# One core, two layers of mixers and feed-forward: the last mixers in two streams before retention, the second output projection in block pairs, operand sums on POOL, another pool order

## The chip, the cores and the metric

The kernel runs on one core of a Trainium2 chip. The metric is device time in microseconds, the median of several runs. One execution of the program is also profiled; its trace gives every instruction's start and duration. TensorE is called PE, VectorE DVE, ScalarE ACT, GpSimd POOL and SyncE SP. SP issues most of the transfers; the code of the other engines sees them through semaphores.

## The reference

Two layers over 1024 tokens of width 1024. A layer is four token mixers side by side, an output projection, and a gated feed-forward with a causal convolution over three tokens:

```python
h = rms_norm(x, g_pre_mix)
p = h @ w_in
a_pool, r_q, r_k, r_v, r_g, s_u, s_v, d_qkv, d_z, d_b, d_a = jnp.split(p, IN_SPLITS, axis=-1)
y_a = pool_mixer(a_pool, pool_w, pool_scale)
y_b = retention_mixer(r_q, r_k, r_v, r_g, cos, sin)
y_c = spatial_gating_mixer(s_u, s_v, sgu_ln_g, sgu_ln_b, sgu_ws, sgu_bs)
y_d = deltanet_mixer(d_qkv, d_z, d_b, d_a, dn_conv_w, dn_a_log, dn_dt_bias, dn_norm_g)
y = jnp.concatenate([y_a, y_b, y_c, y_d], axis=-1)
x = x + rms_norm(y @ w_out, g_post_mix)
h = rms_norm(x, g_pre_ffn)
x = x + rms_norm(conv_ffn(h, ffn_w_up, ffn_conv_w, ffn_conv_b, ffn_w_down), g_post_ffn)
```

Retention multiplies queries and keys (turned by rope) within chunks of 128 tokens and carries a state from chunk to chunk. The delta-net solves a unit lower triangular system of 64 tokens for each chunk and head, and carries a state through the chunks. Both are short dependent chains of small products; the projections, up and down are large products.

## The kernel before

All is in float32. A large product is made of three products of rounded parts: an operand is split into hi (a cast, on ACT) and lo (the difference, on DVE), and hi x hi, hi x lo and lo x hi are added in PSUM. A weight tile of 512 KB is loaded into one of two raw buffers and split by `unit` (L187 to L202). `a_unit` multiplies it with the transposed rows of 512 tokens in 24 matmuls (L210 to L212); `b_units` uses two such weight tiles for four blocks of 128 tokens (L231 to L233).

The tokens are taken in two halves of 512. The order of all instructions on each engine is fixed beforehand by the framework's scheduler, which simulates the program; `high_priority` shifts what it wraps towards an earlier place in that order. An engine then takes its instructions one by one: one that waits holds all behind it on this engine, and SP's transfers the same.

The part of the program that matters here begins with the last mixers, those of layer 1 and the second half of the tokens.

- `win` runs the projections and mixers in the order of the letters in ORD: among others u (the projections of retention's q, k, v), n (retention's gate), r (retention) and b (the delta-net's end).
- `retention` turns q and k by rope (DVE L630 and L634, POOL L633), then runs four blocks with the state `ret`. With FAST for the first mixers of the program (layer 0, first half) it runs two blocks by turns.
- `dn_back` inverts the triangular 32 x 32 parts: 31 steps on DVE, each a product and a sum (L831, L833), a transfer to memory and back (SP L835 to L866), then for each of four blocks a solve (L874 to L912) and a scan (L936 to L961). Without FAST solve and scan of a block come one after another; with FAST `turns` lets generators run by turns: two solves together, then scans 0 and 1 beside solves 2 and 3, then scans 2 and 3.
- `plain_up` makes up tiles f = 0 to 7 of layer 1 for the first half of the tokens: five before the output projection and three behind it. Its rows are transposed and split by `to_hT` (L365 to L369).
- `out` projects the mixers' output by `wO`, and `norms` adds the residual, norms again and stores the result to `hnD`.
- `build` loads rows from `hnD`, makes the seven transposed operands A11, A12, A22, S1, S2, S3, Q4 of a product scheme with seven instead of eight block products; one call takes one half of the tokens. `up_f` then makes an up tile with seven products, for one half (256 columns) or both. f = 0 to 7 are made for the second half alone, since `plain_up` made the first. Up tiles go to memory in `gD`.
- `down_full` loads them again (`graw`), splits them, loads the down weights (raw, `in_wD`), and adds up all in `acc`; `end_block` norms a block, adds x (`xb`, issued by POOL at L1207) and stores it.

`phase` opens the tile pools of a part of the program; a pool of a later phase that lies where an earlier one lay waits for that one's tiles. So the order of the pools sets which old tile a new one waits for.

Of the kernel before, what the change touches and what calls it, by code (L numbers as in the profile page):

```python
# [9 lines left out]
F32 = mybir.dt.float32  # L10
# [4 lines left out]
ALU = mybir.AluOpType  # L15
# [18 lines left out]
ORD0 = "unszrpqgfb"  # L34
ORD = "zspgqunrb"
HP0 = {"r": 500, "b": 300}
HP1 = {}
# [79 lines left out]
class Net:  # L117
# [30 lines left out]
    def down_phase(self):  # L148
        self.phase(("pw", 6), ("pg", 6), ("pa", 8), ("pr", 2), ("py", 2))

# [70 lines left out]

    def b_units(self, aps, hT, width, n):
        us = [self.unit(ap, 4 * width) for ap in aps]
        for b in range(NB):
            ps = self.ps()
            for k in range(len(hT)):
                hi, lo = us[k // 4]
                s = slice((k % 4) * width, (k % 4 + 1) * width)
                tb = slice(b * P, b * P + P)
                h0, h1 = hT[k][0][:, tb], hT[k][1][:, tb]  # L230
                self.nc.tensor.matmul(ps[:, :width], h0, hi[:, s], start=k == 0, stop=False)  # L231
                self.nc.tensor.matmul(ps[:, :width], h0, lo[:, s], start=False, stop=False)  # L232
                self.nc.tensor.matmul(ps[:, :width], h1, hi[:, s], start=False, stop=k == len(hT) - 1)  # L233
            yield b, ps
# [72 lines left out]

    def norms(self, raw, hn, gpost, gpre, src, dst, keep=None):
        nc = self.nc
        for b in range(NB):  # L310
            xb = self.py.tile([P, D], F32, tag="xb", name="xb")
# [106 lines left out]
    def win(self, l, h, hT, pre=None):  # L418
# [105 lines left out]
        def do_ret():  # L524
            self.retention(l, h, R["rqk"], R["rv"], R["rg"], FAST and (l, h) == (0, 0))

        def do_back():
            self.dn_back(l, qf, R["zf"], sc, dn, FAST and (l, h) == (0, 0))

# [3 lines left out]
        steps = dict(n=do_rg, f=do_first, z=do_z, s=do_su, p=do_pool, g=do_sgu, q=do_pmix, u=do_runits, r=do_ret, b=do_back)  # L533
        for k in (ORD0 if (l, h) == (0, 0) else ORD):
            off = dict(HP0 if (l, h) == (0, 0) else HP1).get(k)
            if off:
                with self.tc.high_priority(offset=off):
                    steps[k]()
            else:
                steps[k]()  # L540
# [424 lines left out]
    def out(self, l, h, y, mid=False, halves=False):  # L965
# [18 lines left out]
        gpost = self.bcast(t["gB"][4 * l + 1], "zf" if mid else "gpost", pool=alt if mid else None)  # L984
        gpre = self.bcast(t["gB"][4 * l + 2], "ap" if mid else "gpre", pool=alt if mid else None)
        for kh in range(2 if halves else 1):
            for q in range(4):
# [4 lines left out]
                for b, ps in self.b_units(aps, yT[4 * kh:4 * kh + 4 * len(aps)], 256, 4):  # L992
                    with self.tc.high_priority(offset=HPE):
                        if kh == 0:
                            nc.scalar.copy(raw[b][:, s], ps[:, :256])
                        else:
                            nc.vector.tensor_tensor(raw[b][:, s], raw[b][:, s], ps[:, :256], ALU.add)
        hn = raw if mid else self.acc_tiles()
        self.norms(raw, hn, gpost, gpre, src, dst, self.hnD[l][h * HALF:h * HALF + HALF] if l in FULL else None)
        return hn  # L1000
# [28 lines left out]
    def cbuf(self, name):  # L1029
        return self.pu.tile([P, 1028], F32, tag="c", name=name, bufs=4)  # L1030

# [11 lines left out]
    def build(self, l, h):  # L1043
        nc = self.nc
        V, A = nc.vector, self.A
        for i in range(2):
            cs = slice(h * 256 + i * P, h * 256 + i * P + P)
            xs = []
            for e in range(2):
# [3 lines left out]
                xs.append(x)  # L1053
            ps = []
            for e in range(2):
                for kk in range(2):
                    p = self.ps() if kk == 0 else self.pq()
                    for k in range(4):
                        c = (kk * 4 + k) * P
                        nc.tensor.transpose(p[:, k * P:k * P + P], xs[e][:, c:c + P], self.ident)  # L1060
                    ps.append(p)
            p00, p01, p10, p11 = ps
            v4 = lambda a: a.rearrange("p (k t) -> p k t", k=4)

            def put(n, src):
                hi, lo = self.A[n]
                nc.scalar.copy(hi[:, :, cs], v4(src))
                V.tensor_tensor(lo[:, :, cs], v4(src), hi[:, :, cs].bitcast(F32), ALU.subtract)

            a21, s1, s3, s2, q4 = (self.pbuf(n) for n in ("a21", "s1", "s3", "s2", "q4"))  # L1070
            put("A11", p00)
            nc.scalar.copy(a21, p10)
            V.tensor_tensor(s1, a21, p11, ALU.subtract)
            put("S1", s1)
            V.tensor_tensor(s2, s1, p00, ALU.subtract)
            put("S2", s2)
            put("A12", p01)
            V.tensor_tensor(s3, p00, a21, ALU.subtract)
            put("S3", s3)
            V.tensor_tensor(q4, s2, p01, ALU.add)  # L1080
            put("Q4", q4)
            put("A22", p11)

# [118 lines left out]
    def end_block(self, l, b, acc, gpost):  # L1202
        nc = self.nc
        V = nc.vector
        rows = slice(b * P, b * P + P)
        xb = self.py.tile([P, D], F32, tag="xb", name="xb")
        nc.gpsimd.dma_start(xb, self.xs[2 * l][rows])  # L1207
# [92 lines left out]
    def run(self):  # L1300
# [23 lines left out]
        self.build(l, 1)  # L1324
        for f in range(NHALF):
            if f == 1:
                self.build(l, 0)
            self.up_f(l, f, (1,))
        for f in range(NHALF, NF):
            self.up_f(l, f, (0, 1))  # L1330
        self.down_phase()
# [78 lines left out]
```

## Time and profile before

| | us |
|---|---|
| median of 3 runs | 2571.22 (2569.04 to 2571.54) |
| the profiled execution | 2572.25 |
| its span | 2570.5 |
| PE busy | 2444.2 (95%) |
| DVE busy | 1771.3 (69%) |
| ACT busy | 963.6 (37%) |
| POOL busy | 242.7 (9%) |

The span is the time from the first to the last record of the profiled execution. Busy times are sums over the whole span. Times in a timeline are from the span's start: start, duration, engine, line and operation, written and read tiles, and in brackets the idle time before it and what ended it. In groups the two numbers behind the bar are the sum in us and the mean of one in ns.

### The profile page before, as it was taken

The page shows a single profiled execution, that of the slowest core. Times are in us where ns is not written, and L with a number is a line of the kernel's source. Part 1 is how long each engine was busy: PE and PEld are TensorE (multiplying, and loading weights), DVE is VectorE, ACT ScalarE, POOL GpSimd, SP SyncE. Part 2 cuts the span into 40 slices and gives each one's busy share as a digit, 9 for nine tenths or more (in the row PEclk, how much of TensorE's full clock was granted, in tenths as well). Part 3 has the DMA queues.
Part 4 walks back from the last instruction along what each step waited for, and adds up shares of the span by engine and source line. Part 5 has one row for each costly group of instructions (what it writes and reads, how often), then busy time and mean ns, then how long its engine had stood idle before and what let it go on. Part 6 is the DMA issues. An engine that isn't in the chain of part 4 may idle for free. (4 is left out here: it accounts for less than half of the span.)

```text
span 2570.5 us, 36403 instructions
## 1 busy us (share of the span) xinstructions
PE 2444.2 (95%) x14068; PEld 2041.1 (79%) x14068; DVE 1771.3 (69%) x3665; ACT 963.6 (37%) x1505; POOL 242.7 (9%) x343
## 2 busy tenths in 40 slices
PE   8989998999999999999999999896968999989997
PEld 7978987877788978787788897785858888868886
DVE  7895799665655888855655687963388866653537
ACT  6343443423323462433333355231245534433212
POOL 2321112000000014000000001300000000000002
PEclk9999999999999999999999999995899999999999
DMA  5233442322233542322223453230253322233313
GB/s 181 77 90 101 140 143 79 96 72 86 87 91 128 167 148 78 89 75 83 74 91 99 148 189 132 77 104 22 66 201 115 107 86 79 82 108 106 131 66 115
DMA packets 97329, 270.34 MB, mean 105 GB/s; under 512 B 30130, under 2 KB 30450, under 8 KB 96644
## 3 DMA queue, kind: packets, MB, share of 16 engines
q1 hardware_dynamic: 93380, 255.36, 30.5%
q0 software_dynamic: 3776, 12.65, 1.6%
q8 instruction: 111, 1.82, 0.3%
q14 instruction: 62, 0.51, 0.1%
HBM read 230.19 MB, written 37.78 MB: 104 GB/s over the span
## 5 line engine op out<-in xcount | busy, mean ns | idle before, releaser
L200 ACT CAST whi<-raw 128x1024 fp32r<-128x1024 f32 (+1 forms) x290 | 302.3, 1049 | 669.8 <-PE psg L211 193.1
L211 PE MATMUL psg<-hT,whi 128*128 128x512 f32 x1280 | 509.1, 398 | 1.3 <-DVE hT L369 1.3
L210 PE MATMUL psg<-hT,whi 128*128 128x512 f32 x1280 | 508.9, 398 | 0.5 <-DVE hT L369 0.3
L212 PE MATMUL psg<-hT,wlo 128*128 128x512 f32 x1280 | 508.9, 399 | 0.0
L201 DVE TENSOR_TENSOR wlo<-raw,whi 128x1024 fp32r<-128x1024 f32 (+1 forms) x267 | 329.6, 1240 | 180.1 <-ACT whi L200 175.3
L211 PEld LDWEIGHTS psg<-hT,whi 128*128 128x128 f32 x1280 | 241.7, 189 | 57.1 <-DVE hT L369 1.9
L212 PEld LDWEIGHTS psg<-hT,wlo 128*128 128x128 f32 x1280 | 241.8, 189 | 55.8 <-issue 0.2
L210 PEld LDWEIGHTS psg<-hT,whi 128*128 128x128 f32 x1280 | 241.6, 189 | 54.8 <-ACT hT L368 0.6
L1247 DVE TENSOR_TENSOR acc<-acc,psg 128x512 f32<-128x512 f32 x160 | 109.1, 686 | 74.6 <-PE psg L1242 74.0
L232 PE MATMUL psg<-wlo,hT 128*128 128x256 f32 (+1 forms) x512 | 148.5, 291 | 5.9 <-DVE wlo L201 5.9
L231 PE MATMUL psg<-whi,hT 128*128 128x256 f32 (+1 forms) x512 | 145.8, 288 | 3.1 <-DVE rqk L510 3.0
L231 PE MATMUL psg<-whi,y 128*128 128x256 f32 x512 | 144.6, 288 | 4.1 <-ACT y L205 2.2
L233 PE MATMUL psg<-whi,hT 128*128 128x256 f32 (+1 forms) x512 | 148.0, 290 | 0.0
L232 PE MATMUL psg<-wlo,y 128*128 128x256 f32 x512 | 144.8, 285 | 0.0
L1106 ACT CAST w<-wraw 128x512 fp32r<-128x512 f32 x154 | 92.2, 619 | 138.3 <-PE psg L1092 57.7
L233 PE MATMUL psg<-whi,y 128*128 128x256 f32 x512 | 143.7, 285 | 0.0
L1240 PE MATMUL psg<-whi,g 128*128 128x512 f32 x352 | 141.5, 404 | 0.0
L1241 PE MATMUL psg<-wlo,g 128*128 128x512 f32 x352 | 138.8, 394 | 0.0
L1242 PE MATMUL psg<-whi,g 128*128 128x512 f32 x352 | 138.6, 394 | 0.0
L1107 DVE TENSOR_TENSOR w<-wraw,w 128x512 fp32r<-128x512 f32 x154 | 103.6, 688 | 46.5 <-ACT w L1106 45.3
L831 DVE SCALAR_TENSOR_TENSOR pr<-A 64x1 f32<-64x1 f32 (+30 forms) x124 | 115.2, 929 | 5.6 <-POOL A L827 3.6
L232 PEld LDWEIGHTS psg<-wlo,hT 128*128 128x128 f32 x512 | 98.1, 192 | 9.7 <-DVE wlo L201 6.9
(464 smaller groups left out, 5095.3 us busy)
## 6 DMA issues: line engine op xcount, KB each, us to landing
raw<-in_wU SPq DMA_DIRECT2D x104, 512.0 KB, 3.5
raw<-in_wD SPq DMA_DIRECT2D x66, 512.0 KB, 3.7
raw<-in_wA SPq DMA_DIRECT2D x56, 512.0 KB, 3.7
wraw<-in_wU SPq DMA_DIRECT2D x22, 1024.0 KB, 4.9
raw<-in_wO SPq DMA_DIRECT2D x32, 512.0 KB, 3.7
raw<-in_wB SPq DMA_DIRECT2D x24, 512.0 KB, 3.6
xs<-xb SPq DMA_DIRECT2D x24, 512.0 KB, 3.4
graw<-gD SPq DMA_DIRECT2D x22, 512.0 KB, 4.8
```

The costliest lines, as they stand in the source:

```text
L200: nc.scalar.copy(hi[:, :n], raw[:, :n])
L201: eng.tensor_tensor(lo[:, :n], raw[:, :n], hi[:, :n].bitcast(F32), ALU.subtract)
L210: nc.tensor.matmul(ps, a[0], b[0], start=first, stop=False)
L211: nc.tensor.matmul(ps, a[0], b[1], start=False, stop=False)
L212: nc.tensor.matmul(ps, a[1], b[0], start=False, stop=last)
L231: self.nc.tensor.matmul(ps[:, :width], h0, hi[:, s], start=k == 0, stop=False)
L232: self.nc.tensor.matmul(ps[:, :width], h0, lo[:, s], start=False, stop=False)
L233: self.nc.tensor.matmul(ps[:, :width], h1, hi[:, s], start=False, stop=k == len(hT) - 1)
L831: V.scalar_tensor_tensor(pr[:, 0:i, 0:i], A[:, 0:i, 0:i], -1.0, A[:, 0:i, i].unsqueeze(1).to_broadcast([64, i, i]), ALU.mult, ALU.mult)
L1240: nc.tensor.matmul(ps, hi[:, tb], us[i][0][:, s], start=i == 0, stop=False)
L1241: nc.tensor.matmul(ps, hi[:, tb], us[i][1][:, s], start=False, stop=False)
L1242: nc.tensor.matmul(ps, lo[:, tb], us[i][0][:, s], start=False, stop=i == len(g0) - 1)
```

## The change

- The mixers of layer 1, second half, run in the order ORD1, with b (the delta-net's end) ahead of r (retention), and both take the FAST path (two streams), as the first mixers do. In this path the scans use another PSUM pool and keep their small matrices in row buffers.
- The `out` call that stands between the plain up tiles (`mid`) runs in two passes over block pairs: blocks 0 and 1 through all weights, their norms, then blocks 2 and 3 through all weights again, and their norms. The weights are loaded and split once for each pass.
- `build` computes the four sums on POOL from the loaded rows (128 x 512 each, in buffers of its own), transposes all seven operands on PE instead of four quarters, and splits each from PSUM. The row buffers `c` are six, not four.
- f = 0 and f = 1 are made for the second half, then the other half is built, and f = 2 to 7 for the second half come between the whole tiles from f = 8 on.
- The pools of the down phase are opened in another order, `xb` of the end has six buffers, and the scratch memory for POOL's transfers is 8192.

Line numbers behind the changed lines move by a few: the delta-net's L874, L936 and L960 are L876, L938 and L962 now, the sums on POOL are L1068 to L1071, the split in `build` is L1080, and L1222 of `end_block` is L1220.

```diff
+ORD1 = "zspgqunbr"
+QUICK = ((0, 0), (1, 1))
...
     def down_phase(self):
-        self.phase(("pw", 6), ("pg", 6), ("pa", 8), ("pr", 2), ("py", 2))
+        self.phase(("pa", 8), ("pr", 2), ("py", 2), ("pw", 6), ("pg", 6))
...
-    def b_units(self, aps, hT, width, n):
+    def b_units(self, aps, hT, width, n, blocks=range(NB)):
         us = [self.unit(ap, 4 * width) for ap in aps]
-        for b in range(NB):
+        for b in blocks:
...
-            self.retention(l, h, R["rqk"], R["rv"], R["rg"], FAST and (l, h) == (0, 0))
+            self.retention(l, h, R["rqk"], R["rv"], R["rg"], FAST and (l, h) in QUICK)
...
-            self.dn_back(l, qf, R["zf"], sc, dn, FAST and (l, h) == (0, 0))
+            self.dn_back(l, qf, R["zf"], sc, dn, FAST and (l, h) in QUICK)
...
-        for k in (ORD0 if (l, h) == (0, 0) else ORD):
+        for k in (ORD0 if (l, h) == (0, 0) else ORD1 if (l, h) in QUICK else ORD):
...
+        if mid:
+            for blocks in ((0, 1), (2, 3)):
+                for q in range(4):
+                    for b, ps in self.b_units([t["wO"][l, 2 * q], t["wO"][l, 2 * q + 1]], yT, 256, 4, blocks):
+                        with self.tc.high_priority(offset=HPE):
+                            nc.scalar.copy(raw[b][:, q * 256:q * 256 + 256], ps[:, :256])
+                self.norms(raw, hn, gpost, gpre, src, dst, keep, blocks)
+            return hn
...
     def cbuf(self, name):
-        return self.pu.tile([P, 1028], F32, tag="c", name=name, bufs=4)
+        return self.pu.tile([P, 1028], F32, tag="c", name=name, bufs=6)
...
+            L, R = slice(0, 512), slice(512, 1024)
+            sa, sb = self.cbuf("sa"), self.cbuf("sb")
+            G = nc.gpsimd
+            G.tensor_tensor(sa[:, L], xs[1][:, L], xs[1][:, R], ALU.subtract)
+            G.tensor_tensor(sa[:, R], sa[:, L], xs[0][:, L], ALU.subtract)
+            G.tensor_tensor(sb[:, R], sa[:, R], xs[0][:, R], ALU.add)
+            G.tensor_tensor(sb[:, L], xs[0][:, L], xs[1][:, L], ALU.subtract)
+            for i_, (n, x, s) in enumerate((("A11", xs[0], L), ("A12", xs[0], R), ("A22", xs[1], R), ("S1", sa, L),
+                                            ("S2", sa, R), ("S3", sb, L), ("Q4", sb, R))):
+                p = (self.ps, self.pq)[i_ % 2]()
+                for k in range(4):
+                    nc.tensor.transpose(p[:, k * P:k * P + P], x[:, s][:, k * P:k * P + P], self.ident)
+                p4 = p.rearrange("p (k t) -> p k t", k=4)
                 hi, lo = self.A[n]
-                nc.scalar.copy(hi[:, :, cs], v4(src))
-                V.tensor_tensor(lo[:, :, cs], v4(src), hi[:, :, cs].bitcast(F32), ALU.subtract)
-            a21, s1, s3, s2, q4 = (self.pbuf(n) for n in ("a21", "s1", "s3", "s2", "q4"))
-            put("A11", p00)
-            nc.scalar.copy(a21, p10)
-            V.tensor_tensor(s1, a21, p11, ALU.subtract)
-            put("S1", s1)
...
+                nc.scalar.copy(hi[:, :, cs], p4)
+                V.tensor_tensor(lo[:, :, cs], p4, hi[:, :, cs].bitcast(F32), ALU.subtract)
...
-        xb = self.py.tile([P, D], F32, tag="xb", name="xb")
+        xb = self.py.tile([P, D], F32, tag="xb", name="xb", bufs=6)
...
-        for f in range(NHALF):
-            if f == 1:
-                self.build(l, 0)
+        for f in range(2):
             self.up_f(l, f, (1,))
+        self.build(l, 0)
+        half = list(range(2, NHALF))
         for f in range(NHALF, NF):
+            if half:
+                self.up_f(l, half.pop(0), (1,))
             self.up_f(l, f, (0, 1))
...
-    nc = bacc.Bacc("TRN2", target_bir_lowering=False, num_devices=1)
+    nc = bacc.Bacc("TRN2", target_bir_lowering=False, num_devices=1,
+                   dynamic_dma_scratch_size=8192)
```

PE at the delta-net, before: the last matmul of the first block's solve (L908), its scan, and the next block's solve. Ahead of these rows stand retention and five plain up tiles.

```order
L908 MATMUL psm<-R_14590,kt 64x64
L936 MATMUL psm<-S,tmp 64x64 x8
L951 MATMUL psm<-Sb,qf 64x128 x2
L954 MATMUL psm<-R_14590,AT 128x64 x2
L951 MATMUL psm<-Sb,qf 64x128 x2
L954 MATMUL psm<-R_14590,AT 128x64 x2
L960 MATMUL psm<-ident,tmp 128x128 x2
L874 MATMUL psm<-x_100,LT 32x32 x8
L882 MATMUL psm<-XT,x_100 32x32 x8
```

PE at the same place now: behind the last projection (L213, L214) and a few transposes of the rows for the plain up tiles, the first two solves begin together.

```order
L213 MATMUL psg<-hT_13390,whi 128x512
L214 MATMUL psg<-hT_13388,wlo 128x512
L367 MATMUL psg<-ident,acc_13475 128x128
L367 MATMUL psg<-ident,acc_13476 128x128 x4
L367 MATMUL psg<-ident,acc_13477 128x128 x4
L876 MATMUL psm<-x_99,LT 32x32 x8
L876 MATMUL psm<-x_100,LT 32x32 x8
L884 MATMUL psm<-XT,x_99 32x32 x8
L884 MATMUL psm<-XT,x_100 32x32 x8
L893 MATMUL psm<-R_14590,XT 128x128 x8
```

And where it ends: the last scan, the other transposes, retention's first transposes and scores (L645, L653), then the first plain up matmuls (L212).

```order
L938 MATMUL psh<-S,mc_15467 64x64 x8
L953 MATMUL psh<-Sb,qf 64x128 x2
L956 MATMUL psh<-R_14590,AT 128x64 x2
L953 MATMUL psh<-Sb,qf 64x128 x2
L956 MATMUL psh<-R_14590,AT 128x64 x2
L962 MATMUL psh<-ident,tmp 128x128 x2
L367 MATMUL psh<-ident,acc_13475 128x128 x4
L367 MATMUL psh<-ident,acc_13476 128x128 x4
L645 MATMUL psm<-ident,rqk_14975 128x128 x4
L367 MATMUL psh<-ident,acc_13477 128x128 x4
L645 MATMUL psm<-ident,rqk_14975 128x128 x4
L367 MATMUL psg<-ident,acc_13478 128x128 x4
```

The whole delta-net has moved ahead of retention and of all plain up tiles, and between its solves and scans no matmul of a plain up tile is left.

SP at the first builds, before: the last rows' store (L322), the first build's four loads, two weight loads, the second build's four.

```order
L1101 DMA wraw<-in_wU 128x2x1024
L1026 DMA gD_109<-c 128x512
L1101 DMA wraw<-in_wU 128x2x1024
L322 DMA hnD_107<-osu 128x1024
L1052 DMA hn<-hnD_107 128x1024 x4
L1101 DMA wraw<-in_wU 128x2x1024 x2
L1052 DMA hn<-hnD_107 128x1024 x4
L1164 DMA gD_109<-c 128x512
```

Now:

```order
L324 DMA hnD_107<-osu 128x1024
L1099 DMA wraw<-in_wU 128x2x1024 x2
L1037 DMA gD_109<-c 128x512
L1063 DMA hn<-hnD_107 128x1024 x2
L1099 DMA wraw<-in_wU 128x2x1024
L1063 DMA hn<-hnD_107 128x1024 x2
L1099 DMA wraw<-in_wU 128x2x1024
L1162 DMA gD_109<-c 128x512
L1063 DMA hn<-hnD_107 128x1024 x2
L1099 DMA wraw<-in_wU 128x2x1024
L1162 DMA gD_109<-c 128x512
```

The rows' stores stand before the last plain up tile's store; the loads come in pairs, with a weight load between them, and the second build's behind the first split tiles' stores.

SP from up to down, before:

```order
L1177 DMA graw<-gD_109 128x1024 x2
L1164 DMA gD_109<-c 128x1024
L198 DMA raw<-in_wD 128x1024 x2
L1177 DMA graw<-gD_109 128x1024 x2
```

The first down weights have moved behind two more loads of `graw`:

```order
L1175 DMA graw<-gD_109 128x1024 x2
L1162 DMA gD_109<-c 128x1024
L1175 DMA graw<-gD_109 128x1024 x2
L200 DMA raw<-in_wD 128x1024 x2
L1175 DMA graw<-gD_109 128x1024 x2
```

More of the change, by code (lines that the diff above doesn't have):

```diff
@@ L306, in sumsq, with norms @@
         return self.rstd(ss, 1, 1.0 / D)
-    def norms(self, raw, hn, gpost, gpre, src, dst, keep=None):
+    def norms(self, raw, hn, gpost, gpre, src, dst, keep=None, blocks=range(NB)):
         nc = self.nc
-        for b in range(NB):
+        for b in blocks:
             xb = self.py.tile([P, D], F32, tag="xb", name="xb")
@@ L985, in out @@
         gpre = self.bcast(t["gB"][4 * l + 2], "ap" if mid else "gpre", pool=alt if mid else None)
+        hn = raw if mid else self.acc_tiles()
+        keep = self.hnD[l][h * HALF:h * HALF + HALF] if l in FULL else None
+        if mid:
[6 more added lines that the diff above has]
+            return hn
         for kh in range(2 if halves else 1):
@@ L997, in out @@
                             nc.vector.tensor_tensor(raw[b][:, s], raw[b][:, s], ps[:, :256], ALU.add)
-        hn = raw if mid else self.acc_tiles()
-        self.norms(raw, hn, gpost, gpre, src, dst, self.hnD[l][h * HALF:h * HALF + HALF] if l in FULL else None)
+        self.norms(raw, hn, gpost, gpre, src, dst, keep)
         return hn
@@ L1053, in build @@
                 xs.append(x)
[L1054 to L1065, printed above, removed]
-                hi, lo = self.A[n]
-                nc.scalar.copy(hi[:, :, cs], v4(src))
-                V.tensor_tensor(lo[:, :, cs], v4(src), hi[:, :, cs].bitcast(F32), ALU.subtract)
-            a21, s1, s3, s2, q4 = (self.pbuf(n) for n in ("a21", "s1", "s3", "s2", "q4"))
-            put("A11", p00)
-            nc.scalar.copy(a21, p10)
-            V.tensor_tensor(s1, a21, p11, ALU.subtract)
-            put("S1", s1)
[L1075 to L1082, printed above, removed]
+            L, R = slice(0, 512), slice(512, 1024)
[11 more added lines that the diff above has]
+                p4 = p.rearrange("p (k t) -> p k t", k=4)
+                hi, lo = self.A[n]
+                nc.scalar.copy(hi[:, :, cs], p4)
+                V.tensor_tensor(lo[:, :, cs], p4, hi[:, :, cs].bitcast(F32), ALU.subtract)
     def product(self, ps, a, b, cs, first, last):
```

## The prediction

> **What bounds the kernel now.** I read the page first, then busy time in 20 us stretches, then single instructions where PE is not full. In the page the first line is the span.
>
> ```profile
> span 2570.5 us, 36403 instructions
> PE 2444.2 (95%) x14068; PEld 2041.1 (79%) x14068; DVE 1771.3 (69%) x3665; ACT 963.6 (37%) x1505; POOL 242.7 (9%) x343
> ```
>
> PE is the bound; it is idle 126 us in all. The profiled execution took 2572.25 us, 1.75 more than its span and 1.0 above the median of the runs; the sum below is made against 2572.25, and 1.0 comes off at the end. The orders of both kernels are the same up to about 1520 us, so only what follows can move. The stretches there (PE, PEld, DVE, ACT, POOL busy; then PE's clock, the DMA share, GB/s):
>
> ```profile
> 1660.00:1680.00 20.00, 14.84 (x71) 12.18 (x70) 19.86 (x26) 6.05 (x11) 0.00 (x0) 0.83 0.25 79
> 1740.00:1760.00 20.00, 12.81 (x132) 10.29 (x134) 9.16 (x30) 2.57 (x8) 1.05 (x4) 0.67 0.13 42
> 1760.00:1780.00 20.00, 13.14 (x122) 10.01 (x122) 6.30 (x23) 2.30 (x7) 3.35 (x12) 0.50 0.02 3
> 1900.00:1920.00 20.00, 6.08 (x37) 5.67 (x38) 16.46 (x34) 10.42 (x19) 0.19 (x1) 0.74 0.85 315
> 1920.00:1940.00 20.00, 13.43 (x93) 12.32 (x92) 18.49 (x32) 9.89 (x19) 0.00 (x0) 0.91 0.17 55
> 1940.00:1960.00 20.00, 14.83 (x99) 14.44 (x100) 17.31 (x30) 12.26 (x24) 0.37 (x2) 0.83 0.34 117
> 2300.00:2320.00 20.00, 11.10 (x39) 8.90 (x40) 12.27 (x12) 11.66 (x14) 0.00 (x0) 0.74 0.85 292
> ```
>
> So there are three holes: the last delta-net (1740 to 1820, half clock), the start of the split up projection (1900 to 1960, 25.7 us idle, DVE nearly full), and the step from up to down (2300). The tail is a fourth. Each part of the change aims at one.
>
> **Part A, last mixers.** The delta-net's chain of 31 steps on DVE, its loads, the retention's end, and the delta-net's blocks, from the timeline:
>
> ```profile
> 1616.01 0.90 DVE L831 SCALAR_TENSOR_TENSOR pr<-A 64x1 f32<-64x1 f32 x1
> 1685.06 1.15 DVE L833 TENSOR_REDUCE A<-pr 64x31 f32<-64x961 f32 x1
> 1694.87 1.77 SPq L866 DMA_DIRECT2D x<-d  x4
> 1662.65 0.49 PE L651 MATMUL psm<-tmp 64*128 64x128 f32 x4
> 1747.98 0.65 PE L874 MATMUL psm<-x,LT 128*32 128x32 f32 x16
> 1756.29 0.69 PE L936 MATMUL psm<-S,tmp 64*64 64x64 f32 x8
> 1765.12 0.69 PE L960 MATMUL psm<-ident,tmp 128*128 128x128 f32 x2 [3.50 <-DVE tmp L617]
> 1765.74 0.64 PE L874 MATMUL psm<-x,LT 128*32 128x32 f32 x16
> 1823.38 0.41 PE L960 MATMUL psm<-ident,tmp 128*128 128x128 f32 x2 [1.00 <-DVE tmp L617]
> 1865.74 0.28 PE L233 MATMUL psg<-whi,y 128*128 128x256 f32 x1
> 1865.85 0.39 PE L210 MATMUL psg<-hT,whi 128*128 128x512 f32 x1
> 1866.08 0.39 PE L211 MATMUL psg<-hT,whi 128*128 128x512 f32 x1
> ```
>
> From 1662.65 (first matmul that hangs on retention) to 1865.85 (the output projection is done) PE needs 203 us. Before, retention and five plain up tiles stand ahead of the delta-net, so its loads, there at about 1699 (issue 1694.87 + 1.77 + some 2.2), wait until 1748. After, PE has nothing between the last projection and the delta-net.
>
> The chain gets shorter, since rope and transposed-row work of DVE moves behind it:
>
> ```profile
> L630 DVE TENSOR_TENSOR tmp<-rqk,rope 128x512 f32<-128x512 f32 x4 | 3.3, 813 | 0.0
> L634 DVE TENSOR_TENSOR rqk<-tmp 128x512 f32<-128x512 f32 x4 | 3.2, 808 | 0.6 <-POOL tmp L633 0.6
> L369 DVE TENSOR_TENSOR hT<-psg,hT 128x512 fp32r<-128x512 f32 x4 | 2.6, 674 | 0.0
> L369 DVE TENSOR_TENSOR hT<-psh,hT 128x512 fp32r<-128x512 f32 x4 | 2.5, 674 | 0.0
> L633 POOL TENSOR_TENSOR tmp<-rqk,rope 128x256 f32<-128x256 f32 x32 | 41.3, 1312 | 27.9 <-DVE rqk L510 21.5 <-issue 5.2 <-DVE tmp L575 1.0
> ```
>
> That is 3.3 + 3.2 + 2.6 + 2.5 = 11.6 us, with some 2 us of slow steps beside POOL 13.6; the chain ends at 1686.2 - 13.6 = 1672.6, the loads are there 12.6 later, at 1685. SP issues the same ten small DMAs, in nearly the same order. PE waits 1663.4 to 1685: 21 us (17 if its other inserted work goes too, 32 if the chain does not shorten).
>
> The delta-net: a solve takes 1756.29 - 1747.98 = 8.3, a scan 1765.74 - 1756.29 = 9.4, all 17.7 a block one after another. In two streams: two solves side by side 8.3 + 2.7 for the second's matmuls = 11, scan 0 with solves 2 and 3 between its steps 9.4 + 7, then three scans 28.2: 56 us (71 if nothing overlaps, 49 if the solves vanish behind the scans). Before the four took 76 (1748 to 1824), with the first output matmuls in their gaps; now nothing fills them, as the order lets no plain up matmul in.
>
> Behind it stand what left the chain: 11.6 us on DVE, with POOL's eight rope products (8 x 1.31 = 10.5) beside it; DVE's share of the last scan hides a little: 11 until PE is fed (3 to 14). Then ten units of 24 matmuls at 0.23 (1866.08 - 1865.85) = 56, with four retention blocks, 12: 68. Half clock at its start is within that. The output projection is 384 matmuls at 0.12 = 45.
>
> Its block pairs load and split all weights twice: 8 more loads, 8 more casts, 8 more differences on DVE, each used for half the matmuls (2.8 us a unit):
>
> ```profile
> raw<-in_wO SPq DMA_DIRECT2D x32, 512.0 KB, 3.7
> L200 ACT CAST whi<-raw 128x1024 fp32r<-128x1024 f32 (+1 forms) x290 | 302.3, 1049 | 669.8 <-PE psg L211 193.1
> L201 DVE TENSOR_TENSOR wlo<-raw,whi 128x1024 fp32r<-128x1024 f32 x4 | 4.9, 1225 | 0.7 <-ACT whi L200 0.6
> ```
>
> With two raw buffers a unit comes every (3.7 + 1.05 + 1.2) / 2 = 3.0, against 2.8 of PE; 16 x 0.2 = 3, less what is loaded ahead: 2 (0 to 6). The first pair's norms then run under the second pair; before they ran under the last three up tiles, which also hid all but the last.
> Sum of A: 21 + 56 + 11 + 68 + 45 + 2 = 203, against 203: **0** (-15 to +20 with the bounds above, which will not all fall on one side).
>
> **Part B, start of the split up projection.** From the plain up tiles' end T = 1899.2:
>
> ```profile
> 1903.65 6.45 SPq L1052 DMA_DIRECT2D hn<-hnD  x4
> 1911.06 1.09 PE L1060 MATMUL psg<-ident,hn 128*128 128x128 f32 x4 [11.83 <-DVE w L1107]
> 1948.31 1.09 PE L1060 MATMUL psg<-ident,hn 128*128 128x128 f32 x4 [2.16 <-ACT S2h L1067]
> L1073 DVE TENSOR_TENSOR s<-a,psm 128x512 f32<-128x512 f32 x4 | 2.7, 683 | 0.9 <-issue 0.8 <-ACT a L1072 0.2
> L1215 POOL TENSOR_TENSOR gx<-acc,gpost 128x512 f32<-128x512 f32 x8 | 10.7, 1340 | 243.2 <-DVE acc L1197 228.1 <-DVE rs L276 6.5 <-DVE rs L284 4.7
> ```
>
> Before: steady at about T + 50, with only f = 0 done. After: the normed rows are stored early, the first loads go out at T + 1.3 and land at T + 6; four sums on POOL cost 4 x 1.34 = 5.4. The second pair of loads sits on SP behind a weight load that waits for DVE (T + 10), lands at T + 16, sums until T + 21. 28 sets of four transposes replace 16: 48 more matmuls, some 5 us, in time that is idle. DVE loses 16 sums, 16 x 0.683 = 10.9. Two half tiles (84 matmuls x 0.12 = 9.8 each) are done by T + 41; then the second build waits for loads behind these tiles' stores, and PE is steady at T + 54, one half tile ahead: 54 - 50 - 9.8 = -6. POOL beside DVE takes 2 of that back (see the third rival): **-4** (-14 to +8). Half tiles between whole ones afterwards spread DVE's load; PE idles about 1.2 us there now: **-1** (0 to -1.5).
>
> **Part C, up to down.** The timeline at the step:
>
> ```profile
> 2304.66 0.89 SPq L1177 DMA_DIRECT2D graw<-gD  x2
> 2308.90 0.79 PE L1190 MATMUL psm<-whi,g 128*128 128x512 f32 x1 [10.23 <-ACT whi L200]
> ```
>
> PE waits 10.23 for the first down weights' cast. With the other pool order SP holds two more loads of g, which wait for DVE's splits of the first two, ahead of these weights: 0.9 of issue, and 1 MB first in the engines at 292 GB/s, up to 3.4. **+3** (0 to +5).
>
> **Part D, tail.** The last block waits for x:
>
> ```profile
> 2565.79 1.41 DVE L1222 SCALAR_TENSOR_TENSOR xb<-gx,rs,xb 128x512 f32<-128x512 f32 x2 [2.92 <-DMA xb<-xs]
> ```
>
> With six buffers this load need not wait for a store: **-3** (0 to -4). The halved scratch for POOL's DMAs meets only 15 of these here, spread out: 0.
>
> Sum: 0 - 4 - 1 + 3 - 3 = -5; 2572.25 - 5 - 1 = **2566**.
>
> **Rivals.** *Slower: the delta-net stands bare.* If the two streams do not overlap on the chip (each step waits for ACT or DVE, and both streams share these), it takes 71, not 56: +15, **2580**. For it: clock 0.50 and PE's short steps at 1760 to 1780, with DVE a third busy, so latency counts. Against: DVE and ACT are mostly free. It decides when the delta-net ends after about 1752.
> *Faster: build two hides.* If PE goes from f = 1 into a second build that is ready, steady work begins at T + 44: another -10, **2557**. For it: six row buffers where there were four. Against: SP's order has those loads behind the stores of f = 0 and f = 1.
> *The sums on POOL relieve nothing.* One POOL product and the DVE steps beside and behind it:
>
> ```profile
> 1650.75 2.41 POOL L201 TENSOR_TENSOR wlo<-raw,whi 128x1024 fp32r<-128x1024 f32 x1 [3.11 <-ACT whi L200]
> 1650.85 3.26 DVE L831 SCALAR_TENSOR_TENSOR pr<-A 64x484 f32<-64x484 f32 x1
> 1654.83 1.15 DVE L831 SCALAR_TENSOR_TENSOR pr<-A 64x529 f32<-64x529 f32 x1
> ```
>
> The step beside POOL's 2.41 us took 2.1 more than the larger one behind it: 0.9 us lost per us of POOL. 16 sums are 21.4 us of POOL; if DVE's casts and adds meet all of them it loses 19, not the 10.9 it gave away: B goes from -4 to +3, **2573**. Against: many fall in DVE's waits.
> The Trainium skill has this as a rule: its page "Trainium Architecture — The Big Picture", section "What this means for kernel authors", says the port pair that VectorE and GpSimd share is locked exclusively, not split. The rows agree for the step shown; by the rule this rival would be the rule and not the exception.
>
> **How the numbers follow.** Forecast 0.30 (its own range 2557 to 2576), bare delta-net 0.28, build two hidden 0.27, no relief 0.15. A measurement of this kernel can tell about 0.2%, 5 us: faster is below 2566, slower above 2576. Faster: 0.16 + 0.01 + 0.26 + 0.01 = 0.44; same: 0.12 + 0.07 + 0.01 + 0.08 = 0.28; slower 0.28. Range 2545 to 2588: from build two hidden with A 12 better, to the bare delta-net with A 8 worse.
>
> **What would show it.** A: PE idle from about 1663 to 1685, first L876 near 1685, last L962 near 1740, first plain up matmul near 1751, output projection ending near 1866. B: steady products 54 us after the last plain up matmul. C: first down matmul 13 us after the last up matmul. D: no wait of L1220 for x. The forecast is wrong where the delta-net ends past 1752 or before 1730, or where the holes of B last as long as now.

## The result, and the profile after

The changed kernel takes 2557.47 us, the kernel before 2570.65 in the same comparison: a ratio of 0.995, with a 95% interval of 0.9933 to 0.9967. That is 13 us faster, where 5 had been forecast; the time lies inside the stated range. The profiled execution took 2557.02 us. The head of its page:

```profile
span 2555.2 us, 36529 instructions
PE 2431.4 (95%) x14116; PEld 2031.3 (79%) x14116; DVE 1773.3 (69%) x3657; ACT 968.4 (38%) x1509; POOL 267.0 (10%) x359
```

PE works 13 us less by the record of busy time and waits 2.5 us less. Less busy does not mean fewer matmuls: it made 48 more. At half clock a matmul counts longer: in the changed kernel a plain up matmul began every 0.43 us from 1737 to 1741 (clock 0.50) and every 0.23 us from 1742 on. The stretches show where the half clock lies now (PE, PEld, DVE, ACT, POOL busy; clock, DMA share, GB/s):

```profile
1660.00:1680.00 20.00, 5.04 (x78) 4.43 (x78) 8.26 (x8) 3.50 (x7) 2.60 (x5) 0.59 0.40 93
1680.00:1700.00 20.00, 16.91 (x314) 13.74 (x313) 13.54 (x46) 6.25 (x18) 4.17 (x13) 0.99 0.09 29
1700.00:1720.00 20.00, 10.99 (x68) 7.79 (x68) 10.10 (x36) 1.79 (x4) 5.75 (x12) 0.52 0.00 0
1720.00:1740.00 20.00, 14.82 (x53) 11.33 (x54) 16.19 (x32) 6.30 (x12) 5.04 (x7) 0.50 0.09 34
1740.00:1760.00 20.00, 20.00 (x102) 16.52 (x101) 11.06 (x37) 5.57 (x9) 0.00 (x0) 0.95 0.21 65
1900.00:1920.00 20.00, 14.93 (x101) 13.86 (x101) 15.57 (x23) 9.50 (x19) 8.35 (x8) 0.74 0.29 106
1920.00:1940.00 20.00, 14.92 (x126) 14.55 (x126) 16.83 (x32) 10.03 (x19) 0.00 (x0) 0.91 0.47 164
1940.00:1960.00 20.00, 17.07 (x104) 14.30 (x103) 12.57 (x20) 10.44 (x20) 10.83 (x11) 0.92 0.22 74
2280.00:2300.00 20.00, 6.84 (x22) 5.10 (x22) 11.58 (x11) 8.36 (x8) 3.06 (x6) 0.70 0.77 282
```

The hole of the delta-net now lies at 1660 to 1740, ahead of retention, and from 1740 on PE is full. The two holes behind it are still there: the start of the split up projection and the step from up to down.

The delta-net in the timeline of the changed kernel: the last sum of the chain, the loads, the first solve, the first scan, the last scan's transpose, the first plain up matmul, and the first and last matmuls of the output projection.

```profile
1666.62 1.15 DVE L835 TENSOR_REDUCE A<-pr 64x31 f32<-64x961 f32 x1
1669.75 0.45 SPq L846 DMA_DIRECT2D d<-A  x1
1672.86 6.11 SPq L868 DMA_DIRECT2D x<-d  x8
1675.20 1.42 PE L876 MATMUL psm<-x,LT 128*32 128x32 f32 x32 [14.72 <-DMA x<-d]
1683.65 0.27 PE L938 MATMUL psh<-S,mc 64*64 64x64 f32 x1
1694.35 0.45 PE L938 MATMUL psh<-S,mc 64*64 64x64 f32 x8
1722.11 0.66 PE L962 MATMUL psh<-ident,tmp 128*128 128x128 f32 x2 [5.50 <-DVE tmp L619]
1733.74 1.65 PE L212 MATMUL psg<-hT,whi 128*128 128x512 f32 x3 [0.67 <-ACT hT L370]
1806.06 0.28 PE L233 MATMUL psg<-whi,y 128*128 128x256 f32 x1
1852.82 0.28 PE L235 MATMUL psg<-whi,y 128*128 128x256 f32 x1
1853.56 0.50 PE L212 MATMUL psg<-hT,whi 128*128 128x512 f32 x1 [0.46 <-ACT whi L202]
```

The output projection ends at 1853, 12.9 us earlier than before. What PE did in the parts of the delta-net, by the columns of the stretches above: first, in the kernel before, the solve of one block;

```profile
1747.98:1756.29 8.31, 6.05 (x81) 5.04 (x81) 1.85 (x5) 1.16 (x4) 0.40 (x2) 0.50 0.03 4
```

then, in the changed kernel, the first two solves side by side, and the first scan with the other two solves between its steps:

```profile
1675.20:1683.65 8.45, 8.21 (x141) 7.28 (x142) 3.07 (x8) 2.25 (x8) 0.79 (x4) 0.69 0.07 12
1683.65:1694.35 10.70, 10.05 (x221) 8.38 (x218) 7.72 (x27) 5.19 (x15) 2.36 (x7) 1.00 0.02 4
```

Two streams fill PE here, and its granted clock is higher. The step from up to down and the tail in the changed kernel:

```profile
2282.39 0.39 PE L1090 MATMUL psg<-A22h,w 128*128 128x512 f32 x1
2287.10 0.32 SPq L1162 DMA_DIRECT2D gD<-c  x1
2288.20 1.46 SPq L1175 DMA_DIRECT2D graw<-gD  x2
2289.70 0.90 SPq L200 DMA_DIRECT2D raw<-in_wD  x2
2294.83 1.04 ACT L202 CAST whi<-raw 128x1024 fp32r<-128x1024 f32 x1 [0.21 <-DMA raw<-in_wD]
2295.93 0.80 PE L1188 MATMUL psm<-whi,g 128*128 128x512 f32 x1 [13.16 <-ACT whi L202]
2547.16 1.41 DVE L1220 SCALAR_TENSOR_TENSOR xb<-gx,rs,xb 128x512 f32<-128x512 f32 x2
2550.47 1.41 DVE L1220 SCALAR_TENSOR_TENSOR xb<-gx,rs,xb 128x512 f32<-128x512 f32 x2
```

The same step in the kernel before, from the store of the last up tile to the cast of the first down weights:

```profile
2302.99 0.32 SPq L1164 DMA_DIRECT2D gD<-c  x1
2303.35 1.20 SPq L198 DMA_DIRECT2D raw<-in_wD  x2
2307.80 1.04 ACT L200 CAST whi<-raw 128x1024 fp32r<-128x1024 f32 x1 [4.51 <-DMA raw<-in_wD]
```

The wait ahead of the first down matmul has grown from 10.23 to 13.16 us. The weights' loads are now issued 2.6 us behind that store instead of 0.4, since SP waits for and issues two loads of g first, and their cast begins 5.1 us behind the issue instead of 4.5: 2.9 in all. The last step on x has no wait for a load any more.

The two traces by stage, each column a difference of times read from the timelines (the output projection by the start of its last matmul; T is the end of the last plain up matmul; the tail runs from PE's last matmul to the end of the span):

| us | before | after | gain |
|---|---|---|---|
| to the end of the output projection | 1865.7 | 1852.8 | 12.9 |
| from there to T | 33.5 | 35.6 | -2.1 |
| T to the last up matmul | 399.4 | 394.4 | 5.0 |
| from there to the first down matmul | 10.2 | 13.1 | -2.9 |
| down | 247.4 | 247.9 | -0.5 |
| tail | 14.2 | 11.3 | 2.9 |

The sum is 15.3, as in the spans. Nearly all of what the forecast did not have lies in the first row.

### The profile page after: what moved, and what is told of

Same layout as the page of the kernel before. It is cut to its first block, busy times and chain, and to the rows that moved or that the text cites. A ratio compares the mean times of both kernels' runs of the same rounds, so it can differ in the third digit from the quotient of the medians.

```text
span 2555.2 us, 36529 instructions
## 1 busy us (share of the span) xinstructions
PE 2431.4 (95%) x14116; PEld 2031.3 (79%) x14116; DVE 1773.3 (69%) x3657; ACT 968.4 (38%) x1509; POOL 267.0 (10%) x359
## 5 line engine op out<-in xcount | busy, mean ns | idle before, releaser
L202 ACT CAST whi<-raw 128x1024 fp32r<-128x1024 f32 (+1 forms) x298 | 310.6, 1049 | 679.8 <-PE psg L213 205.4
L212 PE MATMUL psg<-hT,whi 128*128 128x512 f32 x1280 | 510.6, 399 | 2.9 <-ACT whi L202 1.3
L213 PE MATMUL psg<-hT,whi 128*128 128x512 f32 x1280 | 509.0, 398 | 0.2 <-DVE hT L371 0.2
L214 PE MATMUL psg<-hT,wlo 128*128 128x512 f32 x1280 | 508.8, 399 | 0.0
L203 DVE TENSOR_TENSOR wlo<-raw,whi 128x1024 fp32r<-128x1024 f32 (+1 forms) x275 | 338.8, 1237 | 169.5 <-ACT whi L202 165.1
L212 PEld LDWEIGHTS psg<-hT,whi 128*128 128x128 f32 x1280 | 242.1, 189 | 57.5 <-ACT whi L202 1.9
L213 PEld LDWEIGHTS psg<-hT,whi 128*128 128x128 f32 x1280 | 241.8, 189 | 56.0 <-issue 0.6
L214 PEld LDWEIGHTS psg<-hT,wlo 128*128 128x128 f32 x1280 | 241.8, 189 | 55.8 <-issue 0.2
L1245 DVE TENSOR_TENSOR acc<-acc,psg 128x512 f32<-128x512 f32 x160 | 109.0, 686 | 74.7 <-PE psg L1240 74.1
```

Source lines behind the costliest of these rows:

```text
L202: nc.scalar.copy(hi[:, :n], raw[:, :n])
L203: eng.tensor_tensor(lo[:, :n], raw[:, :n], hi[:, :n].bitcast(F32), ALU.subtract)
L212: nc.tensor.matmul(ps, a[0], b[0], start=first, stop=False)
L213: nc.tensor.matmul(ps, a[0], b[1], start=False, stop=False)
L214: nc.tensor.matmul(ps, a[1], b[0], start=False, stop=last)
```

## The experiments

Every kernel is the changed kernel with the edit shown, except where a second edit is named. Each is compared with the kernel before; the changed kernel itself has 0.995 there. Small differences between two of these ratios are to be read with their intervals, 0.0009 to 0.0017 to each side.

| edit | time, us | ratio to before, 95% interval | solves begin | projection ends | T to last up | up to down |
|---|---|---|---|---|---|---|
| changed kernel | 2557.5 | 0.9950 (0.9933 to 0.9967) | 1675.2 | 1852.8 | 394.4 | 13.2 |
| e1: mixers as before | 2572.6 | 1.0006 (0.9997 to 1.0014) | 1747.2 | 1867.0 | 392.8 | 15.3 |
| e2: one pass | 2556.1 | 0.9942 (0.9929 to 0.9955) | 1674.2 | 1849.0 | 396.9 | 14.2 |
| e3: old build | 2552.6 | 0.9926 (0.9914 to 0.9939) | 1676.6 | 1853.0 | 388.0 | 15.5 |
| e4: old pool order | 2561.0 | 0.9960 (0.9948 to 0.9972) | 1677.5 | 1852.9 | 392.5 | 14.7 |
| e5: new order, one stream | 2594.3 | 1.0088 (1.0072 to 1.0104) | 1687.3 | 1889.9 | 392.3 | 16.7 |
| e6: two streams, old order | 2565.1 | 0.9967 (0.9955 to 0.9980) | 1698.8 | 1857.9 | 392.2 | 15.8 |
| e8: old loop | 2561.6 | 0.9962 (0.9948 to 0.9975) | 1673.8 | 1849.9 | 395.4 | 13.8 |
| e9: sums on DVE | 2559.8 | 0.9958 (0.9945 to 0.9970) | 1677.3 | 1853.7 | 392.7 | 16.7 |
| e10: old build, one pass | 2550.5 | 0.9913 (0.9899 to 0.9926) | 1675.4 | 1850.5 | 392.1 | 15.2 |
| e11: e10, old pools, four buffers | 2553.4 | 0.9924 (0.9911 to 0.9936) | 1678.5 | 1854.7 | 393.9 | 13.1 |
| e12: weights' pool last | 2548.1 | 0.9910 (0.9897 to 0.9924) | 1676.1 | 1855.8 | 392.1 | 5.6 |
| e13: e10 with e12's pools | 2543.0 | 0.9888 (0.9874 to 0.9901) | 1673.3 | 1847.9 | 392.2 | 5.6 |

### Which part carries the gain

```diff
-QUICK = ((0, 0), (1, 1))
+QUICK = ((0, 0),)
```

> The changed kernel with the last mixers as before: retention ahead of the delta-net, both in one stream; all else is kept. Theory (the whole gain beyond the forecast is the delta-net's): the output projection ends 13 us later in the trace and the time is 2557.5 + 12.8 = 2570, no different from the kernel before. Rival (the block pairs, by storing normed rows early, or the sums on POOL carry half of it): at most +6, 2563.

With the mixers as before, the whole gain is gone: 1.0006. The other edits together are worth nothing here: the tail gains 2.6, the up phase 6.6, and T comes 4 us later and the step to down costs 5 us more. The theory stands: the gain hangs on the last mixers. This run undoes their order and their two streams at once; the next two part them.

### Order or streams

e5 keeps the new order and takes the second stream away; e6 keeps the two streams and puts retention ahead again.

```diff
 # e5
-  R["rg"], FAST and (l, h) in QUICK)
+  R["rg"], FAST and (l, h) == (0, 0))
-  sc, dn, FAST and (l, h) in QUICK)
+  sc, dn, FAST and (l, h) == (0, 0))
 # e6
-  ORD1 if (l, h) in QUICK else ORD
+  ORD
```

> The changed kernel with the delta-net still ahead of retention, but solves, scans and retention in one stream. Theory (the two streams carry the gain: 47.5 us for the delta-net instead of 71): the delta-net takes 70 us or more from its first solve; plain up matmuls that the order now puts between its steps give part of it back, but the output projection ends at least 8 us later than in the changed kernel: 2565 or more. Rival (the early start carries it, and streams are worth nothing where plain up matmuls fill the gaps): 2555 to 2560.

> The changed kernel with two streams but retention ahead of the delta-net again. Theory (retention's own 12 to 16 us of PE work fit into the 15 us in which PE waits for the chain, and cost only what rope adds to the chain on DVE, some 7 us): loads are there near 1684, the delta-net ends near 1731, the plain up tiles follow without retention between them: the output projection ends 5 to 9 us earlier than in the changed kernel, 2550. Rival (the order is what carries the gain: behind retention the delta-net starts late, as before the change, near 1740): 2570.

The new order in one stream is far slower than the kernel before. Its timeline: the last scan's transpose, then the four transposes that end a retention block.

```profile
1788.06 0.66 PE L962 MATMUL psm<-ident,tmp 128*128 128x128 f32 x2 [5.49 <-DVE tmp L619]
1804.11 0.69 PE L682 MATMUL psm<-ident,tmp 128*128 128x128 f32 x2 [3.44 <-DVE tmp L619]
1814.80 0.69 PE L682 MATMUL psm<-ident,tmp 128*128 128x128 f32 x2 [3.44 <-DVE tmp L619]
1825.49 0.69 PE L682 MATMUL psm<-ident,tmp 128*128 128x128 f32 x2 [3.49 <-DVE tmp L619]
1836.23 0.69 PE L682 MATMUL psm<-ident,tmp 128*128 128x128 f32 x2 [3.49 <-DVE tmp L619]
```

Plain up matmuls did go between the delta-net's first steps, but then they were used up, and retention stood bare: 10.7 us a block, with a wait of 3.4 us for DVE's norm in each. Before, the same retention had lain under plain up tiles. So the order alone moves the bare stretch from one mixer to the other, and the cost is far above the theory's bound of 2565: 2594.

Two streams in the old order gain 7 us against the kernel before (2565.1 us, 0.9967). The theory had 2550 and the rival 2570; neither came. The first solve and the last scan:

```profile
1698.77 1.07 PE L876 MATMUL psm<-x,LT 128*32 128x32 f32 x32
1747.46 0.66 PE L962 MATMUL psh<-ident,tmp 128*128 128x128 f32 x2 [4.41 <-DVE tmp L619]
```

The delta-net itself takes 49 us here, near the changed kernel's 47.6, but it begins at 1698.8 instead of the expected 1684: the chain ends later with rope ahead of it (its first copy is issued at 1677.7, in the changed kernel at 1667.8), and PE has retention's matmuls until the first solve. The projection ends 5 us later than in the changed kernel and 8 earlier than before. So the streams make most of the gain, and the order adds 5 of the 13 at this point once there are two streams.

### The projection in block pairs

```diff
-        if mid:
-            for blocks in ((0, 1), (2, 3)):
...
-                self.norms(raw, hn, gpost, gpre, src, dst, keep, blocks)
-            return hn
```

> The changed kernel with the second output projection in one pass over four blocks, weights loaded and split once. Theory (the double loads are nearly hidden): PE gains at most 2 us in the projection, and loses where the last normed rows are stored about 4 us after the plain up tiles' end instead of 6 us before it: the first build's loads go out 3 to 4 us later; 2557.5 + 2 = 2559.5 (2556 to 2562). Rival (the weights' supply costs what the bound says, 6 us, and the rows are not waited for): 2552.

The projection takes 45.1 us in one pass against 46.8, and T comes 5.9 us earlier (1882.5 against 1888.4); the up phase is 2.5 us longer because the rows come late. The time is 0.9942 against 0.9950: no difference that these intervals can tell, and neither the theory's 2559.5 nor the rival's 2552. In this place the pairs gain nothing, and by the trace they cost about 3.

### The build, and who makes its sums

e3 takes the old `build` back, with its sums on DVE from PSUM; the six row buffers stay. e9 keeps the new one and only moves its four sums to DVE.

```diff
 # e9
-            G = nc.gpsimd
+            G = V
```

> The changed kernel with the build as before (sums on DVE from PSUM, four sets of transposes, row buffers still six). Theory (the sums on POOL gain by taking work off a nearly full DVE): steady products come about 5 us later, 2562.5. Rival (POOL holds DVE up as much as it frees it): no change, 2557 to 2559. Second rival (POOL's sums are themselves waited for by the transposes, 5.4 us in the trace): faster, 2553.

> The changed kernel with the four sums computed by DVE instead of POOL, from the same rows, all else kept (seven sets of transposes, six row buffers). Theory (the build with sums on DVE from PSUM was 6.4 us shorter in the up phase because the transposes no longer wait for POOL's four sums in a row, 5.4 us a pair, and for loads in pairs): each sum takes 0.69 instead of 1.3 us, so a part of it comes back: 2554. Rival (DVE's load is what counts there, and the old build's gain came from fewer transposes and four loads at once): 2558 to 2562, since DVE has 16 sums more.

The old build is better: 0.9926, and 388.0 us from T to the last up matmul. The interval just meets the changed kernel's, but that of e10 further down (0.9899 to 0.9926, old build, one pass) lies below that of e2 (new build, one pass). The number is that of e3's second rival, against the theory; that rival's reason, the wait for POOL, does not hold. With the sums on DVE in the new build the ratio is 0.9958, no different from POOL's, where e9's theory had 2554 us, and the up phase is 392.7 us, like that of the other kernels with the new build, block pairs and the new loop (392.1 to 394.4). So no difference can be told here between the engines that make the sums. What PE waits for in e9, the first rows of the view of its waits from T on (total, times, longest):

```profile
PE psg L1076 <- DMA hn<-hnD: 10.1, 3, 7.3
PE psg L1076 <- DVE sa L1069: 3.6, 2, 2.4
PE psg L1076 <- DVE sb L1070: 2.4, 2, 1.5
```

It waits for the loads, and for the sums one after another, on either engine. In the old build four sets of transposes run first, from the loaded rows alone, and only then the sums follow, from PSUM; there the first products begin 14.0 us after T, in the changed kernel 21.6. In e9 they begin at 15.5, and the up phase is hardly shorter, so the first products alone do not decide: PE then stands before the second build until T + 60.6 in e9 and T + 61.7 in the changed kernel, and until T + 52.7 in e3. That the order of sums and transposes is the cause was read from these waits and not tried by itself.

What POOL does to DVE is seen in the changed kernel. One POOL sum, and what DVE did beside it:

```profile
1899.74 1.72 POOL L1069 TENSOR_TENSOR sa<-sa,hn 128x512 f32<-128x512 f32 x1
1899.12 2.89 DVE L1105 TENSOR_TENSOR w<-wraw,w 128x512 fp32r<-128x512 f32 x2
1901.93 0.68 DVE L1080 TENSOR_TENSOR A22l<-psg,A22h 128x512 fp32r<-128x512 f32 x1
1902.54 1.15 DVE L1109 TENSOR_TENSOR wraw<-wraw 128x512 f32<-128x512 f32 x1
```

Two splits of weights, with both inputs in SBUF, took 2.89 us together (1.21 and 1.75, with a short overlap) where 1.38 is usual (0.69 each), and POOL's sum 1.72 instead of 1.27; a sum of weights took 1.15. The split that reads PSUM took its 0.68 with POOL at work on the next sum. Each of the three slow ones ended 0.54 to 0.56 us after the POOL sum that ran beside it (these ended at 1899.79, 1901.46 and 1903.13), so most of their work seems to have come after it. Over the whole start 27 such splits have a mean of 745 ns and 16 weight sums one of 716 ns: 2 us in all, as the forecast had it, since few of them met.

### The loop

```diff
-        for f in range(2):
-            self.up_f(l, f, (1,))
-        self.build(l, 0)
...
+        for f in range(NHALF):
+            if f == 1:
+                self.build(l, 0)
+            self.up_f(l, f, (1,))
```

> The changed kernel with the old loop over the up tiles: f = 0 for the second half, the other build, f = 1 to 7 for the second half, then the whole tiles. Theory (one half tile ahead of the second build and no spreading of DVE's load cost as in the sum): the up phase is 1 us longer by the spreading and about 3 longer because one half tile less covers the second build's loads: 2561. Rival (the loop gains nothing): 2557.5.

The time is 2561.6 us, 0.9962, with an up phase of 395.4 us. The number is the theory's, but the intervals meet, and the up phase of kernels with the new loop, the new build and block pairs lies between 392.1 and 394.4; so the loop is worth 1 to 3 us, or nothing that can be told.

### From up to down

> The changed kernel with the pools of the down phase opened in the old order. Theory: the first down weights are issued ahead of the third and fourth load of g again, the gap between up and down falls from 13.2 to about 10.2 us and the time by 3, to 2554.5. Rival (with six x buffers the old order makes weights wait for other old tiles): no gain or a loss, 2557 to 2562.

```diff
-        self.phase(("pa", 8), ("pr", 2), ("py", 2), ("pw", 6), ("pg", 6))
+        self.phase(("pw", 6), ("pg", 6), ("pa", 8), ("pr", 2), ("py", 2))
```

The old order did not bring the 3 us back: the wait is 14.7 us. The weights are issued ahead of the third and fourth load of g again, as the theory said, but ACT has a wait in front of their cast:

```profile
2295.39 1.99 ACT L207 CAST g<-graw 128x1024 fp32r<-128x1024 f32 x2 [9.00 <-DMA gD<-c]
2297.29 1.04 ACT L202 CAST whi<-raw 128x1024 fp32r<-128x1024 f32 x1
2298.38 0.79 PE L1188 MATMUL psm<-whi,g 128*128 128x512 f32 x1 [14.73 <-ACT whi L202]
```

The cast of g waits for the store of the last up tile, so the first tile of g lies where the buffer `c` of that tile lay. With SP's order undone the 3 us did not come back, because this other wait stood in the way. Six instead of four such buffers seemed to be its reason. e11 was to show the same from the other side, with four buffers and the old pools:

```diff
-        return self.pu.tile([P, 1028], F32, tag="c", name=name, bufs=6)
+        return self.pu.tile([P, 1028], F32, tag="c", name=name, bufs=4)
```

> As the one with old build and one pass, and also four row buffers and the old pool order of the down phase. Theory (with six row buffers and the old pool order ACT's first cast of g waits for the last store of an up tile, 9.0 us, since the new tile lies where this buffer lay; with four buffers it does not): the gap between up and down falls from 15.5 to about 10.2 us, as before the change, and the time to 2550 - 5 = 2545. Rival (the gap depends on the order of loads on SP, not on where tiles lie): 2549 to 2551.

The wait fell only from 15.2 to 13.1, not to 10.2, and the time did not fall (2553.4, where the theory had 2545). ACT's cast of g still waited 7.35 us for that store, so the six `c` buffers are not its reason, or not the only one. Which of the edits that are left (six x buffers, halved scratch, loop, mixers) puts g over that tile was not tried. So neither edit can be judged by its name; what counts is which old tile a new tile covers. e12 tests that directly, with an order in which the weights' raw tiles lie over tiles that end early:

```diff
-        self.phase(("pa", 8), ("pr", 2), ("py", 2), ("pw", 6), ("pg", 6))
+        self.phase(("pa", 8), ("pr", 2), ("pg", 6), ("py", 2), ("pw", 6))
```

> The changed kernel with another pool order again: rows' buffers of the down phase and x ahead, the down weights' pool last. Theory (where the weights' raw tiles lie sets when they can load): the two first weight tiles then wait for a matmul of the last up tile, not for its end, so they are loaded before PE is done; what is left is ACT's casts of two weights and of g behind the last gelu, about 6 us after the last up matmul instead of 13.2: 2557.5 - 7 = 2550. Rival (the gap is set by the last tile's gelu, store and the loads of g, not by the weights): 2556 or more.

```profile
2272.18 0.33 SPq L200 DMA_DIRECT2D raw<-in_wD  x1
2279.41 0.33 SPq L200 DMA_DIRECT2D raw<-in_wD  x1
2287.75 1.99 ACT L207 CAST g<-graw 128x1024 fp32r<-128x1024 f32 x2
2288.84 0.79 PE L1188 MATMUL psm<-whi,g 128*128 128x512 f32 x1 [5.62 <-ACT g L207]
```

Both weights are loaded before PE has done its last up matmul (2283.2), the wait is 5.62 us, and the time 2548.1: 0.9910 (0.9897 to 0.9924), clear of the changed kernel's interval. This theory is shown: the order of pools alone takes 7.5 us off the wait.

### What beats both kernels

> The changed kernel with the build as before (sums on DVE) and the output projection in one pass; streams, order, loop, pools and six buffers stay. Theory (both edits cost, and independently: 4.4 us of span and 3.0 in the runs with one of them undone): 2557.5 - 7.4 = 2550. Rival (the one-pass projection stores the last rows late, and the old build, which needs all four loads at once, waits for them, where the build with pairs of loads did not): 2553 or more.

> The kernel with the old build and the projection in one pass (2550.5 in its run), with the same pool order as the run before this. Theory: the gap between up and down, 15.2 us there, falls to about 6: 2542. Rival: as above, 2549 or more.

e10 (the edits of e2 and e3 together) has 0.9913, and the up phase is 392.1 us, not 388.0: the first products begin 18.2 us after T instead of 14.0, so the rows that come late in one pass seem to take back what the old build gained, but T is 4.4 us earlier. e13, with e12's pool order, has 2543.0 us and 0.9888 (0.9874 to 0.9901): 28.5 us faster than the kernel before, more than twice what the change gained. The head of its page:

```profile
span 2537.7 us, 36385 instructions
PE 2419.3 (95%) x14068; PEld 2023.1 (80%) x14068; DVE 1768.9 (70%) x3665; ACT 961.7 (38%) x1505; POOL 245.8 (10%) x343
```

Not tried: the old build with block pairs under e12's pool order, the six x buffers alone, and the halved scratch alone. No run holds PE's clock fixed.

## Why the prediction was right or wrong

The direction and the range were right; the size was not, 5 us for 13. The step that was mis-sized is the sum of part A, put at 0 and measured at 12.9 to the end of the output projection. By the forecast's own sign (the delta-net's end before 1730) its account of part A was wrong: it ended at 1722.8.

- **Chain and loads.** The chain's end was put at 1672.6 and the loads at 1685. They were 1667.8 and 1675.2, so the first solve began 10 us earlier than forecast. The loads took 7.4 us behind the chain, not 12.6: in the kernel before SP had weights and a store between these small transfers, and the second copy stood behind the four first reads; now it is issued ahead of them, and all eight last loads follow at once. The price from the old timeline held that queue in it. The other 4.8 us are the chain's: other DVE steps of retention (L656 and L674, 1.3 us) left it too, and the rest is not accounted for.
- **The delta-net.** 56 us were forecast, 47.6 measured (1675.2 to the transpose's end at 1722.8), a little below the lower bound of 49. Two solves side by side took 8.4 us, no more than one had before, and scan 0 with two solves between 10.7, where 11 and 16.4 stood in the sum. The three bare scans took 28, as forecast. The forecast priced the two streams by rows of the kernel before, where the granted clock was 0.50. One solve had PE busy for 6.05 of its 8.31 us there, so two have an estimated 12.1 us of PE work at that clock, which does not fit into the waits of one. In the changed kernel PE was busy for 8.21 of 8.45 us at a mean clock of 0.69, and then for 10.05 of 10.70 us at 1.00; a scan and two solves by the old rows are 5.47 + 12.1 = 17.6 us at half clock, or 8.8 at full. So the second stream filled the first one's waits, and PE, once full, had the higher clock; the sum had the first and left out the second. What the streams would gain at a clock that stays at 0.50 is open. This step gave 8.4 us, of which the plain up tiles take 4 back and the step to T 2.
- **Behind it.** 11 us were forecast until plain up matmuls begin, 11 measured. Plain up and retention: 72.3 for 68, of which half clock until 1741 explains a part. The projection 46.8 for 47.
- **From the projection to T.** The 2.1 us that this stretch grew were not in the sum. Two casts of weights came 0.5 and 0.8 us late; that DVE and ACT were at the second pair's norms is the likely reason, and not tried.
- **Part B.** -5 with the loop, and -5.0 measured, but not by the steps given. Up matmuls can be counted as work (0.117 us each, 0.234 where they are 512 wide). The kernel before had 11.3 us of it done at T + 50 and 23.3 at T + 65, the changed kernel 21.1 and 24.3: the second build of the new form held PE until about T + 62, not T + 54, so the start gained 1 and not 4. By T + 150 it was 104.8 before and 109.5 in the changed kernel: the other 4 came in the half tiles behind. e8 has 109.0 there with the old loop, so the spreading was not it either. What is common to e8 and the changed kernel, and not to the kernel before, is six row buffers among others; with four and the new loop (e11) it was 110.7. What gave these 4 us stays open, so that the size was met here is luck.
- **Part C.** +3 and +2.9, and the changed kernel's trace bears out the reason: SP waits for a split of g and issues two loads of g ahead of the weights, which is 2.2 us of the 2.9, and the weights land 0.7 later behind their issue. But the price is not that of the pool order alone. In e4, with the old order, another wait stands in the same place, and the wait is 13 to 17 us in every kernel with these edits but e12 and e13.
- **Part D.** -3, and -2.9 by the trace; all kernels with six x buffers have a tail of 11.3 to 11.7 us. The buffers were not tried alone.

The rivals. The bare delta-net fell: the streams do overlap. The second build was not hidden; that the measured time is this rival's number, 2557, is chance. That POOL's sums relieve nothing is true in the result (e9, e3), though not for the reason given: DVE lost only 2 us to POOL. The rule of the Trainium skill that stood beside that rival (the page "Trainium Architecture — The Big Picture", section "What this means for kernel authors": a lock on the port, not a split) agrees with the three slow instructions above, which ended just behind the POOL sum beside them; how often they meet was the open number.

## What to carry to other kernels

Where an engine waits through a chain of short dependent steps, two chains by turns can cost hardly more than one: two solves took 8.4 us here and one had taken 8.3. Price the second stream by the waits of the first, and look at the clock of the rows that the price comes from: the one solve ran at a granted clock of 0.50, the two at 0.69. Moving a bare chain ahead of other work only helps if what then stands behind it is not bare itself. Where one phase's tiles reuse another's memory, ask which old tile the first new load covers: another order of pools was worth 7 to 9 us here (e13 against e10, e12 against the changed kernel).

## What was not expected of the hardware

The granted clock did not follow from the busy share of a stretch alone. PE had a granted clock of 0.50 to 0.52 in stretches where it was busy 11 and 14.8 of 20 us, 0.74 in one with 14.9, and 0.99 in one with 16.9; the last one holds two streams of the same short matmuls that ran at 0.50 before. So a bare chain has slower matmuls, too: eight of the scan's (L938) took 0.45 us at 1694 and 0.69 at 1702. A DVE instruction with both inputs in SBUF took 1.75 us instead of 0.69 beside a POOL sum of 1.72 us, while one that read PSUM took its usual 0.68.
